# Head as the innermost loop for the small products of a hybrid decoder layer on one Trainium2 core

## The chip, the cores and the metric

The kernel runs on one core of one Trainium2 chip. The metric is the device time of one execution in microseconds; the kernel before took 2128.84 us (median of three runs, 2128.02 to 2131.24). The engines are named as in the profile: PE is the matrix engine TensorE (PEld are its weight loads), DVE is VectorE, ACT is ScalarE, POOL is GpSimd, and SP is SyncE, which here issues most DMAs.

## The reference

One layer of a hybrid decoder runs over 256 prompt tokens and 8 sequences with one new token each, D = 2048, all in fp32. A SwiGLU feed-forward at half weight stands ahead of the mixing stage and another one behind it; the last step is an RMS norm.

```
x = x + 0.5 * swiglu(rmsnorm(x, n1), f1g, f1u, f1d)
proj = rmsnorm(x, nm) @ w_in
o_att  = attend(q, k, v, sinks)              # 16 query heads of 64, 4 kv heads, window 128, rel. bias, sinks
o_rwkv = rwkv_time_mix(proj[..., ATT_COLS:]) # 16 heads of 64, S_t = S diag(exp lw) + sa kk a^T + v k^T
x = x + concat(o_att, o_rwkv) @ w_out
x = x + 0.5 * swiglu(rmsnorm(x, n2), f2g, f2u, f2d)

def step(S, inp):                            # the recurrence of one head, per token
    sa = einsum('bhij,bhj->bhi', S, -kk_t)
    S = S*exp(lw_t) + sa*(kk_t*a_t) + v_t*k_t
    return S, einsum('bhij,bhj->bhi', S, r_t)
```

The outputs are the tokens of both kinds, the new key and value windows, the recurrent states and the shifted projections.

## The kernel before

**Large products.** Activations lie transposed, 128 features by 264 tokens (256 + 8). Each fp32 weight block of 128 x 512 comes by an SP DMA (`raw`), is rounded by ACT (`hi`, line 122), and the rest is formed by DVE or POOL (`lo`, line 57); `gemm` (line 126) makes three products per 128 x 128 block with them into a bank with tag `acc`. All products are issued by the helper `mm` in line 73, transposes from their own lines, so in the profile the small products of line 73 are told apart by their operands.

**The mixing stage.** `mixing_body` walks through a list: four batches of two head pairs of the recurrence, then keys and values, then the eight tiles of queries (two heads each). Each entry makes the projections (`win`) and spawns tasks, which are Python generators; `tick`, called after each block of a large product, lets every task go on to its next `yield`. So a task's instructions are interleaved with the large products in program order, and the tile scheduler then orders each engine's queue by its own timeline. `drain` runs ticks with no large product between until the tasks that are needed are done; this happens ahead of each of the three passes of the output product (`PASS`: six pairs of the recurrence, the attention, the last two pairs). The first pass also needs the decode path of the recurrence (`dec_rwkv`, `dec_out`).

**The recurrence of 256 tokens** is computed in four chunks of 64 tokens. Two heads share a tile: head 0 has partitions 0 to 63, head 1 partitions 64 to 127 (`HALF`).
- `prep`, one per pair of heads, forms the scaled factors `KR` and `BK` (POOL writes `BK` in halves, one per head), then the Gram blocks `Gm = BK^T KR` (64 rows, 128 columns, 128 wide; profile `m<-kr,bk`), one bank for each head. DVE masks them (`gm`), and SP writes the two diagonal 32 x 32 blocks of each chunk to DRAM (`scr`). Then come the transpose of `KR` (line 432), the products `gv` of `Gm` with the values (`m<-uv,gm`, 64 x 64), and transposes of `BK` (line 446).
- `chain`, one per batch, loads those blocks with 32 rows per partition (`X`, `Y`), and DVE inverts the triangular blocks by substitution (30 steps, rows `st` and `Xt`). They go back through DRAM into `TT`; DVE adds the identity and transposes (`TN`, line 506). Two small 32 x 32 products (`m<-TN,gm`, `m<-TT,zs`) join the inverses to 64 x 64, with an ACT copy of each head between. Then `wus` (`m<-kr,TT`) and `pbs` (`m<-t,W` and `m<-gm,W`), the products `pN` and `pY`, and a loop over the chunks (`m<-N,PT`, `m<-kr,N`, later `m<-S,PT`, `m<-kr,S`), in which the head is already the innermost loop. A normalisation and a gate end the chain.

**The attention**, `attend`, one per query tile: the scores of a head (`m<-s,q`, 64 rows, 256 and 128 wide) go to one bank; DVE adds the bias and takes the maximum (line 721), `softmax` follows on ACT and DVE, then a `yield`, then the same for the other head. The probabilities are transposed (lines 730 to 732) and multiplied by the values (`m<-t,s`).

**Banks.** Three have the tag `acc`, five the tag `m`; the function `mp` hands out the latter in turn, and all small products and transposes use them. The functions as the profile numbers them:

Of the kernel before, what the change touches and what calls it, by code (L numbers as in the profile page):

```python
# [13 lines left out]
P = 128  # L14
# [32 lines left out]
def body(tc, I, O):  # L47
# [46 lines left out]
    with ExitStack() as ctx:  # L94
# [195 lines left out]
        def mixing_body(mx, n2, n3):  # L290
# [60 lines left out]
            def prep(p, bt, k, xrr, xk, xv):  # L351
# [62 lines left out]
                G.tensor_copy(bvdec[:, p, :], bv[:, NP:T])  # L414
                yield
                for h in range(2):
                    r = HALF[h]
                    gp = mp()
                    for c in range(4):
                        mm(gp[:, c * P:(c + 1) * P], BK[r, c, :, :], KR[r, 0:2, c, :])  # L420
                    gm = ring((P, 4, P), "gm", NGM)
                    bt.Gm[k][h] = gm
                    tt(V, gm, gp.rearrange("p (c t) -> p c t", c=4), bc(msk.unsqueeze(1), (P, 4, P)), ALU.mult)
# [13 lines left out]
                gv = mp()  # L437
                for h in range(2):
                    r, o = HALF[h], HALF[1 - h]
                    for c in range(4):  # L440
                        mm(gv[r, c * 64:c * 64 + 64], bt.Gm[k][h][o, c, 0:64], bt.UV[o, c, k, r])
# [21 lines left out]
            def chain(bt):  # L463
# [44 lines left out]
                ps = mp()  # L508
                for h in range(2):
                    for k in range(n):  # L510
                        for c in range(4):
                            j = k * 4 + c
                            mm(ps[h * 64 + 32:h * 64 + 64, j * 32:j * 32 + 32],
                               bt.Gm[k][h][h * 64:h * 64 + 32, c, 32:64], TN[h * 64:h * 64 + 32, j, :])
# [5 lines left out]
                ps = mp()  # L520
                for h in range(2):
                    r = slice(h * 64 + 32, h * 64 + 64)
                    for j in range(4 * n):
                        mm(ps[h * 64:h * 64 + 32, j * 32:j * 32 + 32], zs[r, j, :], TT[r, j, 32:64])
# [9 lines left out]
                for k in range(n):  # L534
                    for h in range(2):
                        r = HALF[h]
                        for c in range(4):
                            mm(wus[k][r, c * P:c * P + P], TT[r, k * 4 + c, :], bt.KR[k][r, 0:3:2, c, :])
# [7 lines left out]
                for k in range(n):  # L546
                    for h in range(2):
                        r = HALF[h]
                        for c in range(1, 4):
                            x = (c - 1) * P  # L550
                            mm(pbs[k][r, x:x + 64], W[r, k, c - 1, :], bt.BT[k][c // 2][r, c % 2, r])
                            mm(pbs[k][r, x + 64:x + P], W[r, k, c - 1, :], bt.Gm[k][h][r, c, 64:128])
                for k in range(n):
# [152 lines left out]
            def attend(t, q):  # L706
# [3 lines left out]
                yield  # L710
                sc = []
                for h in range(2):
                    r = HALF[h]
                    head = (2 * p + h) * 4 + t % 4
                    sps = mp()
                    mm(sps[:, 0:256], q[r, P:NP], kT[p][r, 0:NP])
                    mm(sps[:, 256:384], q[r, 0:P], kT[p][r, 0:P])
                    s1, s0 = tmp((P, 256)), tmp((P, P))
# [293 lines left out]
```

## Time and profile before

| | |
|---|---|
| median of three runs | 2128.84 us |
| the profiled execution | 2127.34 us, span 2125.2 us |
| busy, share of the span | PE 96%, PEld 94%, DVE 63%, ACT 49%, POOL 20% |
| PE records | 16870 |
| granted PE clock, mean | 0.970 |

The first feed-forward fills the span up to about 800 us, the mixing stage lies from there to about 1340, and the rest is the second feed-forward. A record is one matrix instruction; a product of two fp32 operands shows as two. Records are pipelined, so their durations overlap, and what a record occupies is read from one start to the next. A row of the timeline holds the start, the length from the first start to the last end, the engine, the line, the operands, the tile (rows * columns of the array), the shape of the moving operand, the number of records, and in brackets the idle time before it with what ended it.

### The profile page before, as it was taken

What the parts mean: (1) busy time and instruction counts of PE and PEld (TensorE: products, weight loads), DVE (VectorE), ACT (ScalarE), POOL (GpSimd) and SP (SyncE); (2) the same over time, 40 slices, a digit from 0 to 9 for tenths busy, and PEclk for the clock granted to TensorE, in tenths of its full rate; (3) what the DMA queues carried; (4) which work ended last, traced back from release to release, by engine and by line L of the source; (5) the groups of instructions that cost most, each with busy time, mean ns of one, the idle gap of its engine ahead of it and who ended that gap; (6) DMA issues with size and microseconds to landing.
All of it is one profiled execution on the core that took longest, in us unless ns stands there. A gap on an engine that the chain in (4) does not pass through costs nothing.

```text
span 2125.2 us, 45168 instructions
## 1 busy us (share of the span) xinstructions
PE 2043.9 (96%) x16870; PEld 1995.4 (94%) x16870; DVE 1334.3 (63%) x2551; ACT 1045.8 (49%) x2002; POOL 419.5 (20%) x581
## 2 busy tenths in 40 slices
PE   8999999999999999989996899999999999999997
PEld 8999999999999999888885679899999999999997
DVE  5765555556555677766888646755555565555555
ACT  5644444444444566546542344644444444444445
POOL 0301011010201146533454201220110102011012
PEclk9999999999999999989997579999999999999999
DMA  6565565656555574434343145456555565555554
GB/s 224 176 182 182 175 205 175 207 180 183 181 177 185 185 227 139 122 96 135 112 136 114 41 138 186 156 182 181 181 175 187 177 184 181 177 186 176 186 176 140
DMA packets 227532, 356.27 MB, mean 168 GB/s; under 512 B 42176, under 2 KB 83152, under 8 KB 227280
## 3 DMA queue, kind: packets, MB, share of 16 engines
q1 hardware_dynamic: 221616, 344.72, 51.8%
q10 hardware_dynamic: 5696, 8.66, 1.1%
q8 instruction: 132, 2.16, 0.4%
q14 instruction: 88, 0.72, 0.1%
HBM read 345.15 MB, written 10.21 MB: 167 GB/s over the span
## 4 chain that ended last, share of the span: by engine, by line
PE 86%; DVE 7%; DMA 2%; ACT 1%; issue 1%; POOL 1%; SPq 1%; DVEq 0%; POOLq 0%; ACTq 0%
PE acc L73 79%; PE m L73 6%; DVE lo L57 1%; DMA raw<-in_gu 1%; DVE Xt L57 1%; DVE st L57 1%; ACT L67 1%; DVE ld L57 0%; ACT t L67 0%; DMA sb<-Xt 0%; DVE s L60 0%; DVE t L57 0%; DMA TT<-sb 0%; DVE TT L57 0%; DVE t L64 0%
## 5 line engine op out<-in xcount | busy, mean ns | idle before, releaser
L73 PE MATMUL acc<-s,hi 128*128 128x264 f32 x7072 | 1317.5, 286 | 10.0 <-ACT hi L122 8.3
L57 DVE TENSOR_TENSOR lo<-raw,hi 128x512 fp32r<-128x512 f32 (+1 forms) x1266 | 861.7, 684 | 600.6 <-ACT hi L122 578.7
L122 ACT CAST hi<-raw 128x512 fp32r<-128x512 f32 (+2 forms) x1304 | 780.5, 602 | 909.5 <-PE acc L73 830.6
L73 PEld LDWEIGHTS acc<-s,hi 128*128 128x128 f32 x7072 | 1108.8, 190 | 17.8 <-ACT hi L122 8.5
L73 PE MATMUL acc<-s,lo 128*128 128x264 f32 x3536 | 1016.1, 288 | 12.7 <-DVE lo L57 10.5
L73 PEld LDWEIGHTS acc<-s,lo 128*128 128x128 f32 x3536 | 669.9, 189 | 18.5 <-DVE lo L57 14.1
L73 PE MATMUL acc<-t,hi 128*128 128x264 f32 x2752 | 502.7, 284 | 1.6 <-ACT t L251 1.6
L73 PEld LDWEIGHTS acc<-t,hi 128*128 128x128 f32 x2752 | 426.0, 188 | 1.9 <-ACT t L251 1.8
L57 POOL TENSOR_TENSOR t<-t,t 128x264 f32<-128x264 f32 (+1 forms) x162 | 173.0, 1068 | 1209.6 <-ACT hi L122 897.6
L73 PE MATMUL acc<-t,lo 128*128 128x264 f32 x1376 | 388.2, 284 | 0.0
L73 PEld LDWEIGHTS acc<-t,lo 128*128 128x128 f32 x1376 | 258.2, 188 | 0.0
L57 DVE TENSOR_TENSOR t<-acc,t 128x264 f32<-128x264 f32 x164 | 70.9, 433 | 36.7 <-PE acc L73 36.5
L57 POOL TENSOR_TENSOR s<-s,s 128x264 f32<-128x264 f32 (+1 forms) x56 | 49.5, 886 | 195.8 <-ACT s L67 179.1
L57 POOL TENSOR_TENSOR lo<-raw,hi 128x512 fp32r<-128x512 f32 x38 | 49.7, 1308 | 57.4 <-ACT hi L122 57.2
L67 ACT ACT_TABLE_LOAD x42 | 53.9, 1283 | 1.9 <-PEq L1004 1.2
L60 DVE SCALAR_TENSOR_TENSOR s<-acc,s 128x264 f32<-128x264 f32 x96 | 40.7, 428 | 16.8 <-PE acc L73 16.3
L60 DVE SCALAR_TENSOR_TENSOR x<-acc,x 128x264 f32<-128x264 f32 x96 | 40.6, 427 | 10.9 <-PE acc L73 10.4
L57 DVE TENSOR_TENSOR st<-X,Xt 128x60 f32<-128x60 f32 (+10 forms) x120 | 36.1, 300 | 10.1 <-DMA Xt<-sa 7.4
L67 ACT ACTIVATE t<-t 128x264 f32<-128x264 f32 x94 | 40.0, 425 | 3.3 <-DVE t L57 1.8
L57 DVE TENSOR_TENSOR Xt<-Xt,st 128x60 f32<-128x60 f32 (+10 forms) x120 | 36.7, 305 | 1.7
L251 ACT CAST t<-t 128x264 fp32r<-128x264 f32 x86 | 35.5, 413 | 3.6 <-POOL t L57 2.1
L73 PE MATMUL m<-s,hi 128*128 128x264 f32 x160 | 30.1, 287 | 0.4 <-ACT hi L122 0.4
(209 smaller groups left out, 1116.5 us busy)
## 6 DMA issues: line engine op xcount, KB each, us to landing
raw<-in_gu SPq DMA_DIRECT2D x688, 256.0 KB, 3.2
raw<-in_dn SPq DMA_DIRECT2D x224, 256.0 KB, 2.7
raw<-in_win SPq DMA_DIRECT2D x152, 256.0 KB, 3.2
raw<-in_dn SPq DMA_DIRECT2D x160, 192.0 KB, 2.7
raw<-in_wout SPq DMA_DIRECT2D x48, 256.0 KB, 3.0
raw<-in_wout SPq DMA_DIRECT2D x32, 128.0 KB, 2.4
xsp<-x ACTq DMA_DIRECT2D x16, 132.0 KB, 3.5
s<-xsp SPq DMA_DIRECT2D x16, 132.0 KB, 3.0
```

The lines of the kernel that those rows point to most:

```text
L57: return e.tensor_tensor(out=out, in0=a, in1=b, op=op)
L60: return V.scalar_tensor_tensor(out=out, in0=a, scalar=s, in1=b, op0=op0, op1=op1)
L67: return A.activation(out=out, in_=in_, func=f, **k)
L73: TE.matmul(out, lhsT, rhs, start=start, stop=stop, **k)
L122: A.copy(hi[:, :w], raw[:, :w])
L251: A.copy(hi, u)
```

## The change

Seven loops are turned so that consecutive products belong to different heads, that is to different halves of the rows of the array; operands and results stay the same.
- `prep`: the two banks of the Gram blocks are taken together, and the loop over the chunks goes around that over the heads; the masks and DMAs follow in their old order, with the same yields. `gv` likewise.
- `chain`: the two 32 x 32 products, `wus` and `pbs` get the head as the innermost loop; in `pbs` the two operands of a chunk come one after the other, each for both heads.
- `attend`: both heads' banks are taken together and the scores of both are issued ahead of the first softmax: 256 wide for both heads, then 128 wide for both.

```diff
-                for h in range(2):
-                    r = HALF[h]
-                    gp = mp()
-                    for c in range(4):
-                        mm(gp[:, c * P:(c + 1) * P], BK[r, c, :, :], KR[r, 0:2, c, :])
+                gps = [mp(), mp()]
+                for c in range(4):
+                    for h in range(2):
+                        r = HALF[h]
+                        mm(gps[h][:, c * P:(c + 1) * P], BK[r, c, :, :], KR[r, 0:2, c, :])
+                for h in range(2):
                     gm = ring((P, 4, P), "gm", NGM)
...
                 gv = mp()
-                for h in range(2):
-                    r, o = HALF[h], HALF[1 - h]
-                    for c in range(4):
+                for c in range(4):
+                    for h in range(2):
+                        r, o = HALF[h], HALF[1 - h]
                         mm(gv[r, c * 64:c * 64 + 64], bt.Gm[k][h][o, c, 0:64], bt.UV[o, c, k, r])
...
-                for h in range(2):
-                    for k in range(n):
-                        for c in range(4):
+                for k in range(n):
+                    for c in range(4):
+                        for h in range(2):
                             j = k * 4 + c
                             mm(ps[h * 64 + 32:h * 64 + 64, j * 32:j * 32 + 32],
...
-                for h in range(2):
-                    r = slice(h * 64 + 32, h * 64 + 64)
-                    for j in range(4 * n):
+                for j in range(4 * n):
+                    for h in range(2):
+                        r = slice(h * 64 + 32, h * 64 + 64)
                         mm(ps[h * 64:h * 64 + 32, j * 32:j * 32 + 32], zs[r, j, :], TT[r, j, 32:64])
...
-                    for h in range(2):
-                        r = HALF[h]
-                        for c in range(4):
+                    for c in range(4):
+                        for h in range(2):
+                            r = HALF[h]
                             mm(wus[k][r, c * P:c * P + P], TT[r, k * 4 + c, :], bt.KR[k][r, 0:3:2, c, :])
...
-                    for h in range(2):
-                        r = HALF[h]
-                        for c in range(1, 4):
-                            x = (c - 1) * P
+                    for c in range(1, 4):
+                        x = (c - 1) * P
+                        for h in range(2):
+                            r = HALF[h]
                             mm(pbs[k][r, x:x + 64], W[r, k, c - 1, :], bt.BT[k][c // 2][r, c % 2, r])
+                        for h in range(2):
+                            r = HALF[h]
                             mm(pbs[k][r, x + 64:x + P], W[r, k, c - 1, :], bt.Gm[k][h][r, c, 64:128])
...
                 sc = []
+                spp = [mp(), mp()]
                 for h in range(2):
                     r = HALF[h]
+                    mm(spp[h][:, 0:256], q[r, P:NP], kT[p][r, 0:NP])
+                for h in range(2):
+                    r = HALF[h]
+                    mm(spp[h][:, 256:384], q[r, 0:P], kT[p][r, 0:P])
+                for h, sps in enumerate(spp):
                     head = (2 * p + h) * 4 + t % 4
-                    sps = mp()
-                    mm(sps[:, 0:256], q[r, P:NP], kT[p][r, 0:NP])
-                    mm(sps[:, 256:384], q[r, 0:P], kT[p][r, 0:P])
```

More of the change, by code (lines that the diff above doesn't have):

```diff
@@ L415, in prep @@
                 yield
+                gps = [mp(), mp()]
[3 more added lines that the diff above has]
+                        mm(gps[h][:, c * P:(c + 1) * P], BK[r, c, :, :], KR[r, 0:2, c, :])
                 for h in range(2):
-                    r = HALF[h]
-                    gp = mp()
-                    for c in range(4):
-                        mm(gp[:, c * P:(c + 1) * P], BK[r, c, :, :], KR[r, 0:2, c, :])
                     gm = ring((P, 4, P), "gm", NGM)
                     bt.Gm[k][h] = gm
-                    tt(V, gm, gp.rearrange("p (c t) -> p c t", c=4), bc(msk.unsqueeze(1), (P, 4, P)), ALU.mult)
+                    tt(V, gm, gps[h].rearrange("p (c t) -> p c t", c=4), bc(msk.unsqueeze(1), (P, 4, P)), ALU.mult)
                     for blk in range(2):
```

## The prediction

> **What bounds the kernel now.** I read the page first, then the busy times by stage, then the waits of TensorE, then the rows in order of time where TensorE has only small products to do.
>
> ```profile
> span 2125.2 us, 45168 instructions
> PE 2043.9 (96%) x16870; PEld 1995.4 (94%) x16870; DVE 1334.3 (63%) x2551; ACT 1045.8 (49%) x2002; POOL 419.5 (20%) x581
> PE 86%; DVE 7%; DMA 2%; ACT 1%; issue 1%; POOL 1%; SPq 1%; DVEq 0%; POOLq 0%; ACTq 0%
> ```
>
> TensorE is the bound of the whole, and the chain that ended last lies on it for 86%. The change touches only the mixing stage, so the next view cuts that stage in pieces (columns: window and length, busy us of PE, PEld, DVE, ACT, POOL with counts, granted clock, DMA share, GB/s); below the dots stand waits of TensorE (what waited, for what: us in total, times, longest), the lo and gm rows for 800 to 1065 alone, the last two for 1160 to 1245.
>
> ```profile
> 800.00:1065.00 265.00, 245.79 (x2172) 229.78 (x2172) 199.87 (x437) 147.23 (x305) 128.67 (x236) 0.95 0.43 121
> 1065.00:1147.00 82.00, 72.72 (x709) 66.42 (x709) 75.51 (x197) 33.74 (x82) 45.33 (x60) 0.96 0.46 135
> 1147.00:1160.00 13.00, 0.56 (x9) 0.38 (x9) 6.54 (x21) 0.40 (x1) 1.33 (x2) 0.58 0.43 111
> 1160.00:1190.00 30.00, 29.10 (x253) 24.51 (x252) 17.11 (x50) 6.57 (x22) 8.53 (x12) 0.56 0.11 33
> 1170.00:1180.00 10.00, 10.00 (x43) 7.89 (x42) 7.68 (x17) 2.10 (x8) 5.78 (x8) 0.50 0.17 53
> 1199.00:1244.00 45.00, 37.57 (x136) 24.17 (x136) 27.82 (x107) 24.68 (x75) 6.03 (x17) 0.58 0.29 83
> ...
> PE m L73 <- DVE TN L506: 12.4, 1, 12.4
> PE acc L73 <- DVE lo L57: 6.7, 5, 3.1
> PE m L73 <- DVE gm L57: 5.3, 4, 3.1
> PE m L730 <- DVE t L64: 5.0, 3, 2.9
> PE m L73 <- ACT s L594: 4.8, 1, 4.8
> ```
>
> Four regimes are to be seen. From 800 to 1065 TensorE is busy 93%, and its waits (lo, gm) are on VectorE. From 1065 to 1147 VectorE is the bound (75.51 of 82): it runs the last batch's substitution, whose result TN TensorE then awaits for 12.4 us. From 1160 to 1190 no large product is left that may run, and TensorE is busy with small ones at a clock of 0.56. From 1199 to 1244 it alternates with the softmax at 0.58. In this hole of 85 us a microsecond of TensorE is a microsecond of the kernel; before it, only in part.
>
> **What a product costs, head after head and head beside head.** Each fp32 product shows as two records. The starts below tell what one really occupies.
>
> ```profile
> 843.01 1.71 PE L73 MATMUL m<-kr,bk 64*128 64x128 f32 x16
> 844.65 0.44 PE L432 MATMUL m<-C,kr 128*128 128x128 f32 x2
> 961.72 0.96 PE L73 MATMUL m<-uv,gm 64*64 64x64 f32 x16
> 1071.22 1.09 PE L73 MATMUL m<-TN,gm 32*32 32x32 f32 x32
> 928.87 2.56 PE L73 MATMUL m<-kr,TT 64*64 64x128 f32 x32
> 931.37 0.39 PE L73 MATMUL acc<-s,lo 128*128 128x264 f32 x1
> 932.90 0.33 PE L73 MATMUL m<-t,W 64*64 64x64 f32 x2
> 935.30 1.37 PE L73 MATMUL m<-uv,t 128*64 128x64 f32 x29
> 942.78 0.45 PE L73 MATMUL m<-N,PT 64*64 64x64 f32 x8 [2.84 <-DVE Xt L57]
> 943.04 0.43 PE L73 MATMUL m<-kr,N 64*64 64x64 f32 x8
> ```
>
> The loop over c at the end of a batch already has the head innermost: its sixteen records take 942.78 to 943.47, 0.69 us, with starts 33 ns apart (0.26 for eight). The sixteen uv,gm records, same tile size but head after head, take 0.96. So two heads on different halves of the array run at once. I cost an alternating group at half its records times the time of one in a row, plus a tail of 0.2 us (0.35 at half clock).
>
> The Trainium skill speaks against part of this: "TensorEngine Tiling (Array Packing)", section Restrictions and Gotchas, says that different row tiles cannot access the same PSUM bank at once. The trace disagrees for this form, since N,PT puts both heads in one bank, in different partitions, and still starts every 33 ns. By the rule only the Gram products and the scores, which have two banks, would gain; that is the third rival.
>
> **The parts before 1065.** The instructions added and removed are none; only their order changes, and the order that the scheduler makes for the changed kernel can be read off.
> - Gram, per pair of heads 843.01 to 844.65 = 1.64 us. The new order in six of eight pairs is three of head 0, three of head 1, then one and one, because ScalarE and GpSimd finish head 1's factors later; I take 1.25, saving 0.4. Seven pairs lie before 1065: 2.8. Head 0's block ends about when it did, so its mask product on VectorE, its two DMAs on SP and the weight loads behind them there do not start later; head 1's start 0.4 sooner.
> - uv,gm, 0.96 to 0.66, 0.3 times seven: 2.0. The second product now waits for head 1's mask product, with head 0's rest queued behind it. The new order puts the transposes of BK between, which covers that wait; without the cover it costs at most what head 0's rest takes in a row, 0.4.
> - kr,TT, 928.87 to 931.37 = 2.50; 32 records at 0.11 halved give 1.96: 0.5 for two batches, 1.0.
> - W products, 932.90 to 935.30 = 2.40, to 1.6: 0.8 for two batches, 1.6.
> - TN,gm and TT,zs: 32 records in 1.09 are already 32 ns each. Bounds: nothing, if about 30 ns is a floor (alternating starts never come closer than 33), or half, 0.5 a group. I take 0.1 a group, near the first, as the 33 ns row is the nearest: 0.4 for four groups.
>
> Sum 7.8. Where TensorE waits for lo and gm the saving only lengthens the wait; with 12.0 us of such waits in 19 us of idle time I let half pass: 3.9 (bounds 0 and 7.8). From 1065 to 1159 I count nothing, VectorE being the bound; its order of instructions up to TN is nearly unchanged (SP puts the last batch's four writes of the result together, a weight load after them), so the start at 1159.68 moves by what passes before.
>
> **The hole.**
>
> ```profile
> 1159.68 1.03 PE L73 MATMUL m<-TN,gm 32*32 32x32 f32 x16 [12.44 <-DVE TN L506]
> 1160.64 0.47 PE L730 MATMUL m<-C,t 128*128 128x128 f32 x1
> 1161.47 1.65 PE L73 MATMUL m<-s,q 64*128 64x256 f32 x4
> 1163.05 1.05 PE L73 MATMUL m<-TN,gm 32*32 32x32 f32 x16
> 1164.55 1.06 PE L73 MATMUL m<-TT,zs 32*32 32x32 f32 x16 [0.45 <-ACT zs L518]
> 1166.38 1.65 PE L73 MATMUL m<-s,q 64*128 64x256 f32 x4
> 1169.46 3.67 PE L73 MATMUL m<-kr,TT 64*64 64x128 f32 x16 [0.45 <-ACT TT L527]
> 1173.06 1.54 PE L73 MATMUL m<-t,s 128*64 128x256 f32 x4
> 1174.53 3.67 PE L73 MATMUL m<-kr,TT 64*64 64x128 f32 x16
> 1178.13 1.54 PE L73 MATMUL m<-t,s 128*64 128x256 f32 x4
> 1179.60 0.47 PE L73 MATMUL m<-t,W 64*64 64x64 f32 x2
> 1183.81 2.25 PE L73 MATMUL m<-uv,t 128*64 128x64 f32 x29
> 1189.08 0.92 PE L73 MATMUL m<-s,q 64*128 64x256 f32 x4
> 1189.93 0.33 PE L73 MATMUL m<-S,PT 64*64 64x64 f32 x4
> L73 PE MATMUL m<-s,q 64*128 64x256 f32 x24 | 12.5, 617 | 0.0
> ```
>
> Here head 0 and head 1 of the last batch are apart, with attention work between, and every record runs alone at half clock. Step by step:
> - 1159.68 to 1164.55 = 4.87: first TN 0.15, transposes 0.83 (1160.64 to 1161.47), the scores of two heads in place of one (1.58 for one by 1161.47 to 1163.05; 1.8 for two at once), fifteen TN products at 60 ns 0.9 + 0.35, wait 0.45: 4.5. Saves 0.4.
> - 1164.55 to 1169.46 = 4.91: no scores are left here; 0.15 + 0.83 + 1.25 + 0.45 = 2.7. Saves 2.2.
> - 1169.46 to 1179.60 = 10.14, of it 7.2 kr,TT (225 ns a record). 32 records halved at 0.22 plus 0.35 are 3.9, with 2.94 for the products between: 6.85. Saves 3.3.
> - W, 1179.60 to 1183.81 = 4.21; 48 records halved at 0.106 plus 0.35 are 2.9. Saves 1.3.
>
> Together 7.2. Then the scores: the grouped row counts 12 heads in the hole (24 records), two of them used up above. Of the ten, four run at full clock (0.85 each, 1189.08 to 1189.93) and six at half (1.58). As five pairs they take 2 x 1.0 + 3 x 1.8 in place of 3.4 + 9.5: 5.5 saved. In that stretch TensorE is busy 37.57 of 45 us and waits 5.0 for the scaled softmax (DVE t L64), so some of it becomes a longer wait there: I let 0.7 pass, 3.9 (bounds 0 and 5.5).
>
> **Sum.** 3.9 + 7.2 + 3.9 = 15.0 us off the profiled execution's own 2127.3 is 2112.3. The median of the runs is 2128.84, 1.5 above the profiled one, so 2114.
>
> **Rivals.**
> 1. The clock rises too. In the hole two heads at once keep twice as much of the array at work, where from 1170 to 1180 TensorE was busy 10.00 of 10 us with one head at a time and the clock stayed at 0.50. If the fuller array brings the full clock, the 17 us that I left from 1159.68 on shrink by some 7, and what else may pass upstream and in the softmax adds 5 or 6: about 2101. For it: after the products with all rows in use (1183.81) the scores take 0.92 (1189.08) in place of 1.65. Against: kr,TT with two heads uses half the cells, and only one row speaks for it. The Trainium skill, "TensorE: Matmul & The Clock Gate", Part 1, says that the throttle is released after some 3.4 us of sustained activity; the 1170 row disagrees if busy time is what counts.
> 2. The saving is absorbed. Batch 4 is needed only by the last pass of the output product; what the hole ends with is the decode path and the softmax. If upstream passes nothing, the softmax takes back its 3.9 and the wait for ScalarE's s (4.8) grows by half of the 7.2, about 4 us stay: 2125. Against: VectorE is busy only 17.11 of 30 from 1160 to 1190.
> 3. One bank, one tile at a time: only Gram (half of 2.8), the moved score pair (1.4) and the later pairs (3.9) gain, 6.7 us: 2122. This is the skill's bank rule as a mechanism of this kernel; the 33 ns row speaks against it.
> 4. Slower: banks. Products and transposes share five banks of tag m, taken in turn. The score bank of head 1 is now taken together with head 0's, while its reduction still comes a tick of the task list later; 1161.47 and 1166.38 lie 4.9 us apart, so a bank may be held so much longer, and the next product in order stalls. Full price for six pairs in the hole 29, less the 15 gained: 2142. It decides from 2.5 us a pair. Against: in the row of waits none of the large ones is for a bank, and the reductions follow the scores when VectorE is free.
>
> **Chances.** Forecast 0.48 (its own range 2107 to 2120, upstream and softmax passing all or little); clock 0.15; absorbed 0.13, of which 0.08 comes out within 0.2%; one bank 0.10; banks or another order-made wait 0.14. A difference under 0.2%, some 4.3 us, can hardly be told from none. Faster 0.78, same 0.08, slower 0.14. The range 2100 to 2131 leaves out most of the banks' case and the far end of the clock's.
>
> **What would show it.** Right: kr,TT of the last batch as 28 records with starts near 0.11 us at half clock; scores as eight records of a pair in about 1.8 us at half clock, 1.0 at full; Gram groups of about 1.3 us; the wait for TN still about 12 us or longer; the hole, from TN to the return of large products, some 11 us shorter. Wrong: records of alternating heads still 0.22 apart at half clock; a wait for a bank before a transpose; a longer wait for DVE t L64 or ACT s that returns what was saved; half-clock stretches before 1147 where none were.

## The result, and the profile after

The changed kernel takes 2112.05 us (median of four runs, 2108.53 to 2116.84) against 2128.43 us for the kernel before on the same chip (2126.57 to 2131.24). The ratio is 0.9923, with a 95% interval of 0.9908 to 0.9938: 16.4 us faster, where 14.8 were forecast (2114 against 2128.84). A second comparison on another chip gave 2113.89 us and 0.9927 [0.9909, 0.9946]. The sum of the forecast was nearly right. Its parts were not, and the rest of this document is about them.

The execution whose profile was kept first, 2116.84 us, is the longest of its four; a second profile (called "after, second" below, 2113.94 us) is near the median of its six runs. Both are used. First the page of the first one: the span, TensorE's busy time, and the shares of the chain that ended last.

```profile
span 2115.0 us, 45155 instructions
PE 2023.9 (96%) x16870; PEld 1974.8 (93%) x16870; DVE 1330.6 (63%) x2551; ACT 1046.7 (49%) x2004; POOL 424.0 (20%) x581
PE 85%; DVE 8%; DMA 2%; ACT 1%; issue 1%; SPq 1%; POOL 1%; DVEq 0%; ACTq 0%; POOLq 0%
```

The same 16870 records keep TensorE busy 20.0 us less (2043.9 before), and the span is 10.2 us shorter. So about half of the saved work has become a longer wait somewhere.

The hole is cut in three pieces from here on: A from the first TN product of the last batch to the first uv,t product, B from there to the product of the decode result (yr), C from there to the 25th record of the large products that follow (three records for each block of weights; the clock rises about there). Below are the busy times by window (window and length, then busy us of PE, PEld, DVE, ACT and POOL with counts, granted clock, DMA share, GB/s): for the kernel before, pieces A, B, C and the next 200 records of large products.

```profile
1159.68:1183.81 24.13, 23.23 (x166) 19.12 (x166) 14.72 (x42) 5.88 (x20) 8.53 (x12) 0.50 0.13 39
1183.81:1228.49 44.68, 35.05 (x210) 24.46 (x209) 28.99 (x110) 19.71 (x60) 5.42 (x9) 0.61 0.12 36
1228.49:1251.00 22.51, 19.60 (x92) 14.58 (x91) 10.95 (x39) 10.36 (x34) 4.41 (x13) 0.65 0.42 118
1251.00:1283.58 32.58, 32.39 (x321) 30.76 (x321) 18.08 (x45) 15.72 (x38) 4.67 (x12) 0.99 0.60 173
```

For the kernel after, first profile, the same four pieces:

```profile
1156.15:1171.07 14.92, 12.50 (x166) 9.89 (x166) 12.47 (x38) 6.19 (x21) 8.06 (x12) 0.63 0.18 57
1171.07:1212.36 41.29, 29.66 (x208) 19.59 (x209) 28.46 (x106) 18.77 (x58) 6.46 (x11) 0.74 0.15 45
1212.36:1235.18 22.82, 18.33 (x86) 13.64 (x85) 11.82 (x47) 11.62 (x35) 4.30 (x13) 0.65 0.41 115
1235.18:1273.35 38.17, 36.42 (x328) 34.17 (x328) 18.93 (x46) 15.00 (x38) 4.82 (x12) 0.91 0.51 150
```

For the kernel after, second profile, A, B and the same 200 records:

```profile
1158.64:1173.56 14.92, 13.21 (x166) 10.59 (x166) 12.47 (x38) 6.18 (x21) 8.05 (x12) 0.59 0.18 57
1173.56:1212.73 39.17, 25.98 (x208) 17.37 (x208) 28.20 (x105) 17.82 (x53) 6.46 (x11) 0.83 0.15 45
1234.92:1270.37 35.45, 35.12 (x327) 32.80 (x327) 18.20 (x45) 14.89 (x38) 4.65 (x12) 0.94 0.56 159
```

The starts of these windows give the account against the kernel before. In the first profile A begins 3.5 us earlier, A is 9.2 shorter, B 3.4 shorter, C 0.3 longer, and the 200 records of large products behind it take 5.6 longer; that is the 10.2 of the span. In the second A begins 1.0 earlier, A is 9.2, B 5.5 and C 0.3 shorter, and 2.9 are given back: 13.1. More than half of the giving back is the clock: 0.91 and 0.94 in place of 0.99 over 38.17 and 35.45 us are about 3.1 and 1.8 us at full speed. A group of `m<-t,s` (0.8 us) that stood in C before lies there too, and in the first profile one wait of 1.5 us for a load of the decode path (`ld<-in_cv`).

Now piece A in order of time, first profile (start, length, operands, tile, moving shape, records, idle time before):

```profile
1156.14 0.31 PE L73 MATMUL m<-TN,gm 32*32 32x32 f32 x2 [13.43 <-DVE TN L507]
1157.21 1.65 PE L73 MATMUL m<-s,q 64*128 64x256 f32 x8
1158.80 1.05 PE L73 MATMUL m<-TN,gm 32*32 32x32 f32 x30
1160.31 0.31 PE L73 MATMUL m<-TT,zs 32*32 32x32 f32 x2 [0.45 <-ACT zs L519]
1161.38 1.06 PE L73 MATMUL m<-TT,zs 32*32 32x32 f32 x30
1162.88 1.11 PE L73 MATMUL m<-kr,TT 64*64 64x128 f32 x4 [0.45 <-ACT TT L528]
1163.92 1.55 PE L73 MATMUL m<-t,s 128*64 128x256 f32 x8
1165.41 2.53 PE L73 MATMUL m<-kr,TT 64*64 64x128 f32 x26
1167.69 0.27 PE L73 MATMUL m<-t,W 64*64 64x64 f32 x1
1171.07 1.14 PE L73 MATMUL m<-uv,t 128*64 128x64 f32 x16 [1.52 <-DVE uv L544]
```

Two heads now cost what one did: eight score records of a pair take 1.59 us (1157.21 to 1158.80), where four of one head took 1.58. The thirty TN,gm records take 1.05 us from the first start to the last end, as sixteen of one head did before. And there is a gain that the forecast did not see: the probabilities' products `m<-t,s` stood at 1173.06 and 1178.13, one head behind each of the two groups of kr,TT; now both heads stand together and cost 1.49 (1163.92 to 1165.41) instead of 2 x 1.47.

### The profile page after: what moved, and what is told of

Its sections match the earlier page's. It is cut to its first block, busy times and chain, and to the rows that moved or that the text cites. A ratio compares the mean times of both kernels' runs of the same rounds, so it can differ in the third digit from the quotient of the medians.

```text
span 2115.0 us, 45155 instructions
## 1 busy us (share of the span) xinstructions
PE 2023.9 (96%) x16870; PEld 1974.8 (93%) x16870; DVE 1330.6 (63%) x2551; ACT 1046.7 (49%) x2004; POOL 424.0 (20%) x581
## 4 chain that ended last, share of the span: by engine, by line
PE 85%; DVE 8%; DMA 2%; ACT 1%; issue 1%; SPq 1%; POOL 1%; DVEq 0%; ACTq 0%; POOLq 0%
PE acc L73 79%; PE m L73 5%; DVE lo L57 1%; DVE Xt L57 1%; DVE st L57 1%; ACT t L67 1%; DVE ld L57 1%; ACT L67 0%; DMA raw<-in_win 0%; DVE t L64 0%; DVE s L60 0%; DVE t L57 0%; DMA raw<-in_gu 0%; DMA TT<-sb 0%; DVE t L60 0%
## 5 line engine op out<-in xcount | busy, mean ns | idle before, releaser
L73 PE MATMUL acc<-s,hi 128*128 128x264 f32 x7072 | 1320.3, 287 | 17.6 <-ACT hi L122 8.4
L73 PEld LDWEIGHTS acc<-s,hi 128*128 128x128 f32 x7072 | 1112.7, 191 | 25.2 <-issue 9.0
L73 PE MATMUL acc<-s,lo 128*128 128x264 f32 x3536 | 1019.2, 288 | 7.3 <-DVE lo L57 6.5
L73 PEld LDWEIGHTS acc<-s,lo 128*128 128x128 f32 x3536 | 672.2, 190 | 12.7 <-DVE lo L57 9.1
L73 PE MATMUL acc<-t,hi 128*128 128x264 f32 x2752 | 502.7, 285 | 1.6 <-ACT t L251 1.6
L73 PEld LDWEIGHTS acc<-t,hi 128*128 128x128 f32 x2752 | 426.2, 188 | 1.9 <-ACT t L251 1.8
L73 PE MATMUL acc<-t,lo 128*128 128x264 f32 x1376 | 388.6, 285 | 0.0
L73 PEld LDWEIGHTS acc<-t,lo 128*128 128x128 f32 x1376 | 258.5, 188 | 0.0
L67 ACT ACT_TABLE_LOAD x44 | 56.5, 1283 | 2.0 <-PEq L1010 1.2
L67 ACT ACTIVATE t<-t 128x264 f32<-128x264 f32 x94 | 40.0, 426 | 3.1 <-DVE t L57 1.7
L73 PE MATMUL m<-s,hi 128*128 128x264 f32 x160 | 30.1, 287 | 0.1
```

Of the source, the lines that this page charges most:

```text
L67: return A.activation(out=out, in_=in_, func=f, **k)
L73: TE.matmul(out, lhsT, rhs, start=start, stop=stop, **k)
```

## The experiments

The table gathers what all kernels showed. The ratio is to the kernel before on the same chip; A and B are the lengths as above, each from one profile. The last column holds the number of table loads of ScalarE in B and TensorE's wait in the row `PE m L73 <- ACT t L67` there; what they are is told at the kernel with kr,TT undone.

| kernel | ratio, 95% interval | A, us | B, us | TensorE busy and clock in B | table loads in B; wait, us |
|---|---|---|---|---|---|
| before | 1 | 24.1 | 44.7 | 35.1, 0.61 | 4; 1.8 |
| after | 0.9923 [0.9908, 0.9938] | 14.9 | 41.3 | 29.7, 0.74 | 4; 3.3 |
| after, second | 0.9927 [0.9909, 0.9946] | 14.9 | 39.2 | 26.0, 0.83 | 4; 3.7 |
| scores alone | 0.9953 [0.9941, 0.9964] | 20.1 | 36.2 | 25.2, 0.82 | 2; none |
| chain alone | 0.9917 [0.9902, 0.9931] | 15.9 | 40.1 | 32.2, 0.70 | 4; 2.2 |
| prep alone | 0.9981 [0.9972, 0.9990] | 24.1 | 38.4 | 31.8, 0.72 | 2; none |
| all but the scores | 0.9907 [0.9896, 0.9919] | 15.4 | 40.2 | 32.8, 0.69 | 2; none |
| all but the scores, second | 0.9921 [0.9906, 0.9936] | 15.4 | 39.6 | 30.7, 0.73 | 2; none |
| kr,TT and W alone | 0.9959 [0.9944, 0.9975] | 16.2 | 42.2 | 32.5, 0.71 | 4; 1.8 |
| TN,gm and TT,zs alone | 0.9963 [0.9949, 0.9976] | 22.6 | 43.2 | 34.0, 0.66 | 4; 2.0 |
| after, short softmax | 0.9874 [0.9856, 0.9891] | 14.4 | 31.7 | 23.5, 0.84 | 4; 3.0 |
| all but the scores, short softmax | 0.9938 [0.9920, 0.9956] | 15.6 | 41.6 | 32.1, 0.68 | 4; 1.8 |
| after, kr,TT undone | 0.9920 [0.9905, 0.9935] | 19.6 | 33.2 | 23.4, 0.89 | 2; 0.2 |
| all but the scores, t,s turned | 0.9891 [0.9874, 0.9907] | 15.1 | 39.3 | 30.8, 0.77 | 2; none |

**Which part brings the time.** Four kernels on one chip, each with some of the hunks on the kernel before. The first has the scores alone:

```diff
                 sc = []
+                spp = [mp(), mp()]
                 for h in range(2):
                     r = HALF[h]
+                    mm(spp[h][:, 0:256], q[r, P:NP], kT[p][r, 0:NP])
...
-                    sps = mp()
-                    mm(sps[:, 0:256], q[r, P:NP], kT[p][r, 0:NP])
```

> The kernel before with only the attention scores changed (both heads' banks taken together, scores of both heads issued ahead of the first softmax). Theory A (two heads on different row halves run at once, and it pays where TensorE is the bound): a pair of heads' scores takes about 1.6 us at half clock where one head took 1.58, so 6 to 8 us of TensorE are saved in the hole, of which the softmax takes part back: 2121 to 2125. Rival B (the gain comes from the new order of the recurrence's products): no change, 2127 to 2130. Rival C (head 1's bank held longer costs): slower than 2130, with waits of TensorE ahead of a transpose.

Measured: 2120.29 us against 2130.01, 0.9953, just below theory A's 2121 to 2125. That is some 10 us, more than the 3.9 that the forecast gave the scores behind A. Part of it lies in A, which is 4.0 us shorter: both heads' t,s stand together there in this kernel too.

The second has the chain alone (TN,gm, TT,zs, kr,TT and W):

```diff
...
                 for k in range(n):
-                    for h in range(2):
-                        r = HALF[h]
-                        for c in range(4):
+                    for c in range(4):
+                        for h in range(2):
+                            r = HALF[h]
                             mm(wus[k][r, c * P:c * P + P], TT[r, k * 4 + c, :], bt.KR[k][r, 0:3:2, c, :])
...
```

> The kernel before with only the four groups of the chain changed (TN,gm, TT,zs, kr,TT and the W products). Theory A: the stretch from TN,gm to the first uv,t of the last batch shrinks from 24 to 17 us or less, with records of the two heads at half the spacing; upstream of it 1 to 2 us: 2117 to 2121. Rival B (order made by the scheduler, not concurrency): the spacing of kr,TT stays at 0.2 us a record at half clock and the time stays within 3 us of 2128.

Measured: 2112.67 us, 0.9917, below theory A's 2117 to 2121. The chain alone is as fast as the whole change.

The third has the Gram blocks and gv alone:

```diff
-                    gp = mp()
-                    for c in range(4):
-                        mm(gp[:, c * P:(c + 1) * P], BK[r, c, :, :], KR[r, 0:2, c, :])
+                gps = [mp(), mp()]
+                for c in range(4):
+                    for h in range(2):
+                        r = HALF[h]
+                        mm(gps[h][:, c * P:(c + 1) * P], BK[r, c, :, :], KR[r, 0:2, c, :])
...
```

> The kernel before with only the Gram blocks and the gv products changed. Theory A: 16 records of Gram in about 1.3 us in place of 1.64, of gv in 0.66 in place of 0.9 to 1.2, all of it upstream of 1065 us where TensorE often waits for VectorE, so only some of 4.8 us reaches the end, because VectorE is the bound from 1065 to 1147: 2125 to 2128. Rival: nothing is absorbed, 2123 to 2124.

Measured: 2125.96 us, 0.9981: 4 us, within theory A's range. This kernel is also a warning on B: its edit touches no product of A or B, and yet A begins 5.2 us later and B is 6.3 us shorter.

The fourth has everything but the scores (the first diff of this section undone in the changed kernel):

> The changed kernel with the scores as before (prep and chain changed). If the parts add up, the gain is that of e2 plus e3, some 9 to 12 us: 2116 to 2120, and what the changed kernel has on top (2112) is the scores' share, 4 to 7 us. If the parts overlap (one of them alone already removes the same wait), it is 2112 to 2115 or no better than e2.

Measured: 2110.64 us, 0.9907. Chain 17.7, scores 10.0 and prep 4.0 (each one less its ratio, times 2130) would add up to 32; together they give about 16. The parts take the same time off, and the scores on top of the rest add nothing.

**The whole change beside the change without the scores, once more.** Both on one chip.

> The changed kernel again, beside the kernel without its scores part. Theory A (the scores' saving is taken back by the softmax and by the clock once the chain is fast): 2110 to 2114, within 2 us of the kernel without the scores part. Rival B (the first comparison of the two was chance and the parts add up): 4 us or more below it.

> All of the change but the scores, again. Theory A: 2109 to 2113, within 2 us of the whole change. Rival B: 2114 or more, 4 us above the whole change.

Measured: 2113.89 us (0.9927) and 2110.87 us (0.9921). The intervals lie over each other, the medians 3.0 us apart where theory A expected at most 2, and rival B's 4 us in favour of the whole change are not there: nothing measurable is won by the scores on top of the rest. What TensorE does in B differs all the same. The groups of scores in B (256 and 128 wide, eight heads), for all but the scores (second profile) and then for the whole change (second profile):

```profile
L73 PE MATMUL m<-s,q 64*128 64x256 f32 x16 | 8.2, 604 | 0.0
L73 PE MATMUL m<-s,q 64*128 64x128 f32 x16 | 4.2, 352 | 0.0
```

```profile
L73 PE MATMUL m<-s,q 64*128 64x256 f32 x16 | 3.3, 499 | 0.0
L73 PE MATMUL m<-s,q 64*128 64x128 f32 x16 | 1.8, 307 | 0.0
```

The scores cost 12.4 us one way and 5.1 the other, and B is 39.6 and 39.2 us long. All of TensorE's busy time in B is 4.7 us less (30.7 to 26.0), and 4.2 of that have become waiting: TensorE is idle in B for 9.0 us one way and 13.2 the other. The longest waits of TensorE in B of the whole change, second profile:

```profile
PE m L73 <- ACT t L67: 3.7, 1, 3.7
PE m L736 <- DVE t L64: 3.5, 2, 2.5
PE m L73 <- ACT s L597: 3.4, 1, 3.4
```

The first of these rows does not exist in the kernel without the turned scores. It is not a wait for the softmax's VectorE work; what it is comes below.

**The chain in two.** First only kr,TT and W turned, then only the two 32 x 32 products.

```diff
 # first kernel (the rest as before)
                 for k in range(n):
-                    for h in range(2):
-                        r = HALF[h]
-                        for c in range(4):
+                    for c in range(4):
+                        for h in range(2):
+                            r = HALF[h]
                             mm(wus[k][r, c * P:c * P + P], TT[r, k * 4 + c, :], bt.KR[k][r, 0:3:2, c, :])
...
                 for k in range(n):
-                    for h in range(2):
-                        r = HALF[h]
-                        for c in range(1, 4):
-                            x = (c - 1) * P
+                    for c in range(1, 4):
+                        x = (c - 1) * P
+                        for h in range(2):
+                            r = HALF[h]
                             mm(pbs[k][r, x:x + 64], W[r, k, c - 1, :], bt.BT[k][c // 2][r, c % 2, r])
+                        for h in range(2):
+                            r = HALF[h]
                             mm(pbs[k][r, x + 64:x + P], W[r, k, c - 1, :], bt.Gm[k][h][r, c, 64:128])
 # second kernel (the rest as before)
-                for h in range(2):
-                    for k in range(n):
-                        for c in range(4):
+                for k in range(n):
+                    for c in range(4):
+                        for h in range(2):
                             j = k * 4 + c
...
-                for h in range(2):
-                    r = slice(h * 64 + 32, h * 64 + 64)
-                    for j in range(4 * n):
+                for j in range(4 * n):
+                    for h in range(2):
+                        r = slice(h * 64 + 32, h * 64 + 64)
                         mm(ps[h * 64:h * 64 + 32, j * 32:j * 32 + 32], zs[r, j, :], TT[r, j, 32:64])
```

> The kernel before with only the kr,TT and the W products in the new order. Theory A (these carry the chain's gain, by their records and because two heads at once bring the clock up earlier): 2115 to 2120, and in the hole the granted clock reaches 1.0 some 4 to 7 us after the first kr,TT, where it stayed at 0.5 through all of them before. Rival C (only the records count, the clock comes when it comes): 1.3 + 3.3 + 1.3 = 6 us off, 2123 to 2126, with the clock at 0.5 until the uv,t products.

> The kernel before with only the two 32 x 32 products in the new order. Theory A: 0.2 + 2.6 us off, 2126 to 2129, the clock at 0.5 through the kr,TT products as before. Rival D (joining the two heads of the 32 x 32 products, with no attention work between them, carries most of the chain's gain): 2116 to 2121.

Measured: 2120.79 us (0.9959) for kr,TT and W, 2119.47 us (0.9963) for the 32 x 32 products. The first lies between theory A's 2115 to 2120 and rival C's 2123 to 2126, 0.8 us off the former; the second is inside rival D's 2116 to 2121. But piece A bears out other sizes. The 32 x 32 products shorten it by 1.5 (24.1 to 22.6), kr,TT and W by 7.9 (to 16.2), and the two together, the chain alone, by 8.2 (to 15.9). The rest of what the 32 x 32 products show in the total lies outside A: in the profile they begin A 4.6 us earlier, which is no more than edits elsewhere do to the start of A (below).

On the clock theory A holds. The windows from the first kr,TT on, for kr,TT and W alone, up to the point where the clock rises and from there to the first uv,t:

```profile
1166.06:1170.00 3.94, 3.94 (x26) 2.91 (x28) 2.73 (x10) 1.60 (x7) 2.52 (x3) 0.50 0.22 67
1170.00:1172.53 2.53, 2.53 (x66) 2.47 (x63) 2.26 (x6) 1.13 (x4) 1.05 (x3) 1.00 0.15 52
```

For the 32 x 32 products alone, first kr,TT to first W and from there to the first uv,t:

```profile
1163.33:1173.48 10.15, 10.15 (x41) 8.04 (x41) 7.75 (x21) 2.14 (x8) 3.66 (x5) 0.50 0.15 45
1173.48:1177.69 4.21, 4.21 (x50) 4.09 (x49) 1.00 (x3) 0.69 (x2) 2.13 (x3) 0.50 0.12 38
```

TensorE is busy without a gap in both. With two heads at once the clock is at 1.00 after 3.94 us; with one head at a time it stays at 0.50 for 14.36 us. In the turned order the t,s of both heads run together within this stretch, and apart in the other; that alone does not raise the clock, since in the kernel with the scores alone they run together too (1176.29 to 1177.78) and the clock is at 0.50 from 1170.07 to 1181.98. The Trainium skill, "TensorE: Matmul & The Clock Gate", Part 1, puts the rise at around 4 us of sustained activity. The first trace agrees; the second does not, unless one 64 x 64 tile at a time is too little to count as activity.

**Is it the softmax that takes the scores' saving?** The scaling of the exponentials by the reciprocal of their sum is left out, so these two kernels don't compute the reference's attention. One is the whole change, the other all but the scores.

```diff
                 V.reciprocal(sm[:, :n], sm[:, :n])
-                for j in range(n):
-                    ts(V, s[j], s[j], sm[:, j:j + 1], ALU.mult)
```

> The whole change, with the softmax shortened: the scaling of the exponentials by the reciprocal sum is left out (32 VectorE instructions of 0.4 us, 11.5 us in all, in 1100 to 1245). Theory A (with the chain in the new order the softmax is what the scores' saving runs into): the shorter softmax lets the saving through, 3 us or more below the same kernel with the scores head after head, at 2100 to 2107. Rival E (the clock takes it back, or the order of the queue does): within 2 us of it.

> All of the change but the scores, with the same shortened softmax. Theory A: 2104 to 2110. Rival E: the same as with the scores in the new order, within 2 us, whatever both are.

Measured: 2103.74 us (0.9874) with the scores turned, inside theory A's 2100 to 2107, and 2117.17 us (0.9938) without, outside its 2104 to 2110. With a shorter softmax the turned scores are worth 13.4 us, where they were worth nothing. Some 11 of these are what the whole change gains by the shorter softmax (0.9874 against 0.9923 and 0.9927), as theory A has it; the others come from the second kernel, which has become slower. B in the two, the whole change first:

```profile
1168.65:1200.32 31.67, 23.48 (x211) 16.11 (x209) 25.51 (x90) 18.31 (x54) 6.31 (x11) 0.84 0.19 56
```

```profile
1167.27:1208.91 41.64, 32.12 (x211) 22.11 (x209) 25.96 (x97) 18.17 (x54) 5.43 (x9) 0.68 0.17 50
```

With the scores turned, 2.7 us less of VectorE work in B (28.20 to 25.51) shorten it by 7.5; without, 4.5 us less (30.43 to 25.96) lengthen it by 2.0, at a lower clock (0.73 to 0.68). So with the scores turned B follows the softmax, and without them it does not. That the second kernel gained nothing from less work (0.9938 against 0.9907 and 0.9921 with the full softmax) was not expected. It has four table loads in B where the same kernel with the full softmax has two, which can be a part of it; the rest is open.

**kr,TT undone.** The whole change, with kr,TT head after head as before:

```diff
                 for k in range(n):
-                    for c in range(4):
-                        for h in range(2):
-                            r = HALF[h]
+                    for h in range(2):
+                        r = HALF[h]
+                        for c in range(4):
                             mm(wus[k][r, c * P:c * P + P], TT[r, k * 4 + c, :], bt.KR[k][r, 0:3:2, c, :])
```

> The whole change but for the kr,TT products, which go head after head again. Theory A (kr,TT of two heads at once bring the clock up): the granted clock stays at 0.5 through kr,TT and W and rises only some 2.5 us after the first uv,t, W takes some 3 us in place of 1.9, and the time is 5 us or more over the whole change, 2116 to 2120. Rival C (the clock comes when it comes): it rises some 20 us after its last fall in spite of it, and the time is 3 us over the whole change.

Measured: 2113.74 us, 0.9920, the same as the whole change. In order of time:

```profile
1166.43 3.67 PE L73 MATMUL m<-kr,TT 64*64 64x128 f32 x16 [0.45 <-ACT TT L528]
1170.03 1.54 PE L73 MATMUL m<-t,s 128*64 128x256 f32 x4
1171.50 3.67 PE L73 MATMUL m<-kr,TT 64*64 64x128 f32 x16
1175.10 1.54 PE L73 MATMUL m<-t,s 128*64 128x256 f32 x4
1176.58 0.48 PE L73 MATMUL m<-t,W 64*64 64x64 f32 x4
1179.33 1.57 PE L73 MATMUL m<-uv,t 128*64 128x64 f32 x29
```

On the clock theory A is right in the main: it stays at 0.50 up to 1179.33, W takes 2.75 us, the two heads' t,s are apart again, and A is 4.7 us longer. It is at 1.00 from 1180 on, sooner behind the first uv,t than the 2.5 us expected, and some 34 us after it fell (at about 1146), where rival C had 20. On the time it is wrong: no loss is to be seen (0.9920 against 0.9923 and 0.9927), the 5 us are not there, and rival C's 3 us lie at the edge of what the intervals allow. B is 33.2 us in place of 39.2 and 41.3, at a clock of 0.89, and the product of yr starts at 1212.50, where the two profiles of the whole change have it at 1212.36 and 1212.73. What the longer A costs is made good in B. Between these two kernels the sentence on which the forecast's sum rested does not hold, that in this hole a microsecond of TensorE is a microsecond of the kernel.

The chain that ended last says what B is made of. Its shares by line in B, first before, then after (second profile); the view cuts the row off on the right:

```profile
by line: PE m L73 43.8%; ACT L67 8.6%; ACT t L67 7.9%; DVE t L721 4.8%; PE m L730 4.0%; DVE t L624 3.9%; DVE t L64 3.7%; DVE Z L60 2.8%; issue 2.8%; PE m L731 2.2%; PE m L732 2.2%; DVE S L60 1.9%; DVE sta L64 1.5%; DVE ld L57 1.5%; DVE sa L
```

```profile
by line: PE m L73 24.6%; ACT t L67 11.6%; ACT L67 9.8%; DVE t L64 7.2%; DVE t L727 5.9%; DVE t L627 4.5%; issue 4.4%; DVE yr L661 3.1%; DVE Z L60 2.2%; DVE uv L544 2.2%; DVE S L60 2.0%; DVE ld L57 2.0%; ACT stc L67 1.9%; POOL ld L57 1.9%; P
```

TensorE's products fall from 44% to 25% of the chain (36% in the first profile); the rows ACT t, DVE t L64 and the scores' reduction (L721 before and L727 after), most of them the softmax's, rise from 16% to 25%. The row "ACT L67" without operands is this, in B of the second profile (a table load, by which ScalarE changes from one set of functions to another):

```profile
L67 ACT ACT_TABLE_LOAD x4 | 5.1, 1283 | 0.2 <-DVE sta L64 0.2
```

Two of the four stand around one head's exponentials, because ScalarE goes over to the normalisation of a chain (`t<-m,eps`) right behind them. In order of time, with the product of TensorE that follows (second profile; first ScalarE's rows, then TensorE's):

```profile
1192.05 1.28 ACT L67 ACT_TABLE_LOAD   x1 [0.17 <-DVE sta L64]
1193.35 0.51 ACT L67 ACTIVATE t<-t,sta 128x256 f32<-128x256 f32 x1
...
1194.54 1.28 ACT L67 ACT_TABLE_LOAD   x1
1195.83 0.47 ACT L67 ACTIVATE t<-m,eps 128x256 f32<-128x256 f32 x1
```

```profile
1196.36 1.25 PE L73 MATMUL m<-sgl,ld 128*128 128x264 f32 x2 [3.72 <-ACT t L67]
```

The product at 1196.36 uses nothing that this ScalarE instruction writes; what the instruction does is read a bank, `m`. So the 3.72 us are most likely a wait for a bank, held because the bank's reader stands behind the exponentials and two table loads in ScalarE's queue. It is the longest wait in B of this profile, and no score bank is in it. The Trainium skill, "ScalarE: Activation LUTs", What ACT_TABLE_LOAD costs, gives about 1283 ns for a load, whichever set it brings; the trace agrees, with 1283 ns. It adds about 1380 ns for a drain at each change of the set, which this trace does not show: the exponential starts at 1193.35, 0.02 us behind the end of the load.

The kernel with kr,TT undone does not have this wait. Its two instructions of the normalisation stand one behind the other, with a load ahead of them and one behind (`ACT_TABLE_LOAD` at 1193.93 and 1197.53), so there are two loads in B and not four:

```profile
1196.12 0.47 ACT L67 ACTIVATE t<-m,eps 128x256 f32<-128x256 f32 x1 [0.90 <-PE m L73]
1197.04 0.47 ACT L67 ACTIVATE t<-m,eps 128x256 f32<-128x256 f32 x1 [0.45 <-PE m L73]
PE m L73 <- ACT t L67: 0.2, 1, 0.2
```

The last column of the table shows the same in all profiles: with four loads in B TensorE waits 1.8 to 3.7 us behind them, with two at most 0.2. No edit touches ScalarE's work; only the order that the scheduler makes for it differs. So a part of what B of the undone kernel gains, 3.1 to 3.5 us of its 6.0 to 8.1, goes with this order and not with the edit as such, and the same rival stands against the softmax wherever a kernel with four loads is set beside one with two: the whole change beside all but the scores, the scores alone and prep alone beside the kernel before. No run changes that order alone, so its price is not shown. Among kernels with four loads each the finding on the scores stays: with the full softmax the whole change (0.9923, 0.9927) is no faster than the chain alone (0.9917), and with the short one the turned scores are worth 13.4 us.

**One more pair of products turned.** All but the scores, and `m<-t,s` with the head inside:

```diff
                 for h, (pa, pb) in enumerate(pt):
-                    r = HALF[h]
-                    mm(op[r, 0:256], Vt[p][:, 0, r], pa, True, False)
-                    mm(op[r, P:256], Vt[p][:, 1, r], pb, False, True)
+                    mm(op[HALF[h], 0:256], Vt[p][:, 0, HALF[h]], pa, True, False)
+                for h, (pa, pb) in enumerate(pt):
+                    mm(op[HALF[h], P:256], Vt[p][:, 1, HALF[h]], pb, False, True)
```

> All of the change but the scores, and the products of the probabilities with the values turned too (256 wide for both heads, then 128 wide for both; they use the two column halves of the array, 1.47 us a head at half clock in the hole). If column halves run at once as row halves do: 1.5 to 2 us for two heads in place of 2.9, with six or seven pairs in the hole 2104 to 2108. If they don't, or if the second head's later probabilities hold up the first: 2109 to 2115.

Measured: 2107.80 us, 0.9891 [0.9874, 0.9907]. The time is in the faster range, but not for its reason. The group in A before the edit (all but the scores, second profile) and with it:

```profile
1164.26 1.55 PE L73 MATMUL m<-t,s 128*64 128x256 f32 x8
```

```profile
1167.42 1.55 PE L73 MATMUL m<-t,s 128*64 128x256 f32 x8
```

Column halves do run at once, and they already did where one head's products are issued right after the other's. The edit can't gain there, and the profiles of the two kernels end within 0.2 us of each other (2109.61 and 2109.83 us). This is the fastest full kernel of the study, and its interval and that of the whole change don't touch (0.9907 against 0.9908 and 0.9909); they ran on different chips, though, and what would make it faster is not shown.

## Why the prediction was right, and where it was not

- **Upstream, 3.9.** A begins 3.5 and 1.0 us earlier in the two profiles, so the size fits. It can't be called confirmed: the two profiles of one and the same kernel differ by 2.5, with the scores alone (of which only four heads lie ahead of A) A begins 2.2 us later, with prep alone 5.2 later, and with the 32 x 32 products alone 4.6 earlier. These sways are as large as the term or larger. Of its parts, a Gram group takes 1.42 us in the row at 844.20 below, not 1.25, and kr,TT and W ran as costed or faster (thirty-two records of kr,TT 1.9 us in place of 2.50; 1.96 forecast).

```profile
844.20 1.49 PE L73 MATMUL m<-kr,bk 64*128 64x128 f32 x16
845.62 0.44 PE L433 MATMUL m<-C,kr 128*128 128x128 f32 x2
```

- **The hole up to uv,t, 7.2.** Measured 9.2, in both profiles alike. The steps before kr,TT were costed at 2.6; A of the whole change reaches its first kr,TT 3.0 us sooner after TN (6.74 against 9.78), and 1.5 sooner in the kernel with these alone, where a head's scores stand in both gaps. The step kr,TT was mis-sized, 3.3 forecast and 5.3 and 4.9 measured: the 2.94 "for the products between" were left whole, but the two heads' t,s come together and cost 1.49. W was costed at half clock, 2.9 (by 106 ns a record, where 4.21 us for 48 records are 88); at full clock it took about 1.9, but then uv,t waits 1.5 and 0.8 us for VectorE's `uv`, so that this step saves 0.8 and 1.2 of the 1.3 forecast.
- **The scores, 3.9.** This step failed. Their work shrank by more than was costed (12.4 to 5.1 us for four pairs in B, where 5.5 for five pairs were forecast), but the part that becomes waiting is not 0.7: TensorE's busy time in B falls by 4.7 and its waits grow by 4.2. Alone the scores are worth 10 us, on top of the rest nothing. The bounds, 0 and 5.5, held it. What takes the saving is the softmax, as the short softmax shows, and beside it ScalarE's order; the shares are open.
- **The sum.** 15.0 were summed from three terms as if each microsecond counted once. The parts measured alone add up to 32, and the whole gives 16. A reading that fits, but is argued and not shown, is that up to the product of yr the hole has two bounds, TensorE at half clock and the softmax with the decode path, and each part moves it from the one to the other. By place, the two profiles save 3.5 and 1.0 ahead of A (3.9 forecast), 9.2 and 9.2 in A (7.2), 3.1 and 5.8 in B and C (3.9), and lose 5.6 and 2.9 behind (nothing): 10.2 and 13.1, where the forecast had 15.0. That the medians came out 16.4 apart, close to the forecast, is in part luck: a larger A, scores that are absorbed and a loss behind the hole happen to cancel.
- **What was not in the sum.** 2.9 to 5.6 us are given back behind the hole, more than half of it by a clock that falls there (0.94 and 0.91 for 0.99).
- **Rivals.** The clock does rise in part, as the first rival had it, from 4 to 6 us after the first turned kr,TT on, but only until TensorE starts waiting in B, and the 2101 it gave are not reached. The second, absorption, is what happens to the scores, though the time of 2125 that it gave is not reached. The third, one bank and one tile at a time, is refuted: W, TN,gm and kr,TT put both heads in one bank and run at once. The fourth, a held bank, exists with another owner: the 3.72 us above, 1.8 in the profile before by its row for the same instruction (`ACT t L67`), so some 1.5 to 1.9 more in the two profiles (3.3 and 3.7). That is less than what is gained, and the score banks, whose longer hold the rival was built on, are not it.
- **The floor of 30 ns.** TN,gm was taken to be near a floor, which is not there. At half clock thirty records take 1.05 us with their tail, some 28 ns from start to start, and for TT,zs in the first batch, at full clock, the row is as follows: thirty records in 0.69 us with their tail, some 20 ns from start to start.

```profile
923.85 0.69 PE L73 MATMUL m<-TT,zs 32*32 32x32 f32 x30
```

## What to carry to other kernels

Small products of two heads on different halves of the array overlap when they stand next to each other in the queue, whether or not they share a bank. How much that saves is to be measured for each shape: a pair of scores cost as one head, but a Gram group still 1.42 us of 1.64 and kr,TT at full clock 1.9 of 2.50. Look also for groups that other work separates only because a head's loop is outside. Before terms of a stretch are added, ask what bounds the stretch when one of them is gone: here the scores alone were worth more than their share and on top of the rest nothing, and a step of 4.7 us could be undone at no visible loss. Look at the order on the other engines too before a difference is put down to the edit: here two table loads more or fewer came and went with edits that leave ScalarE's work as it is. A saving that leaves the engine waiting can be partly paid back by the clock.

## What the hardware showed that was not expected

- One 64 x 64 tile at a time (with one head's t,s behind each group of kr,TT), TensorE busy for all of 14.36 us, left the clock at 0.50; two tiles at once brought 1.00 after 3.94 us in one kernel, and after 4.2 and 5.7 us in the two profiles of the changed one (1162.88 to 1167.10, 1165.38 to 1171.10).
- Tiles of the two column halves (128 rows, 64 columns) run at once without being interleaved: four records of one head and then four of the other take 1.49 us at half clock, as four of one head alone (1.47).
- The pieces are coupled, and not by the clock alone: the two kernels with turned scores that were slow in A (19.6 and 20.1 us) were short in B (33.2 and 36.2 us) at a clock of 0.89 and 0.82, and the changed kernel, fast in A, was longer there (41.3 and 39.2 us) at 0.74 and 0.83. The two short ones have two table loads in B and the changed kernel four.
- Where ScalarE's two square-root steps of the normalisation stand apart, with a head's exponentials between, each change of the function set costs a load of 1.28 us, and TensorE's wait behind them is 1.8 to 3.7 us in eight profiles; where they stand together it is at most 0.2 in six.
